# Attention values: the second half of the output copied by ScalarE and the sum moved to GpSimd

## The chip, the cores and the metric

The kernel runs on one NeuronCore of one Trainium2 chip. The metric is the device time of one execution in microseconds (us). Its engines are named as in the profile: PE (TensorE; PEld are its weight loads, which overlap the matmuls), DVE (VectorE), ACT (ScalarE), POOL (GpSimd) and SP (SyncE, which here issues DMAs).

## The reference

One layer of a backbone with two branches, on 1024 latent tokens (`x_sample`) and 128 context tokens (`x_prompt`), model width 1024. The change lies in the attention branch, of 8 heads. Each latent token reads 1152 keys (128 cached context keys and 1024 latent ones), and each context token reads the 128 keys of its own sequence:

```
s = einsum('bqhd,bkhd->bhqk', q_nope, k_nope) + einsum('bqhr,bkr->bhqk', q_rope, k_rope)
p = softmax(s.astype(float32) * scale, axis=-1).astype(v.dtype)
return einsum('bhqk,bkhd->bqhd', p, v)
...
y_a = (attn * silu(z_a)) @ w_a_out_l
merged = sigmoid(g_f) * y_f + sigmoid(g_a) * y_a
return x + gate * (merged @ w_out_l)
```

Around it stand the adaLN modulation, the input projection, a Fourier branch, the gated merge, the output projection and a final RMSNorm. All inputs and outputs are fp32.

## The kernel before

**Precision.** A matrix is split into a high and a low part in fp32r (`hi`/`lo`, `th`/`tl`, `kh`/`kl`). `mm3` (L122 to L127) makes a product of three matmuls: high by high (L123), high by low (L126), low by high (L127). The values' matrix V holds both of its parts side by side: `value_map` (L1044) writes the high part into columns 0 to 63 of a head's 128 and the low part into columns 64 to 127. A matmul with it as weights therefore gives 128 rows in PSUM, and rows 0 to 63 and 64 to 127 must be added to give the head's 64 output channels. The changed lines make this sum.

**Stages.** First come the modulation, the Fourier mixing and the input projection, then the Fourier output and the preparation of attention (L1059 to L1102). The attention stage is the loop of L1250 and runs from about 476 to 757 us in the profile. It is followed by the merge with the attention output map (`merge_part`, L1320) and the output projection with the final norm (L1360).

**Attention.** It takes 8 heads and 1152 query columns in 3 groups of 384 (`CH`). For each group and head:

- `q_chunk` (L1029): PE makes the queries, DVE multiplies them by the rotary table (`qf`, L1036), and POOL splits them in two instructions, `hi_pool` (L107) and `lo_pool` (L113), into the tile `q`.
- `Step.score` (L1123): PE makes 128 x 384 scores with `mm3`, DVE takes their minimum (L1131, L1136; scores are kept negated), and ACT makes the exponentials with their sums (`Step.exp`, L1142).
- `Group.trans` (L1155): PE transposes the exponentials (L1163), ACT copies the high part (`th`, L1164), and DVE takes the low part from PSUM (`tl`, L110).
- `Group.values` (L1176): PE accumulates nine key tiles, two matmuls each (L1183, L1184), in one PSUM bank `po`. After the ninth, ACT copies rows 64 to 127 to SBUF (`ob`, L1196) and DVE adds rows 0 to 63 from PSUM (L1197) into the tile `osb`, which two heads share.
- `finish` (L1204), after the odd head of a pair: DVE sums and inverts the softmax sums (L1210, L1212), POOL spreads the inverses over 64 columns in three instructions (L1217) which PE transposes (L1218), DVE multiplies the gate `za` by them (L1219) and by `osb` (L1220), and POOL splits `za` into `ath` (L107) and `atl` (L113). These are read by PE only in the merge.

`k_up` and `k_split` (L1003, L1017) make the next heads' keys in between: PE, two ACT copies (`kf`, L1013), and POOL's two instructions (`kh`, `kl`).

**Order.** The tokens in `HSEQ` (seven heads) and `LSEQ` (the last head) write down the order of scores, exponentials, transposes, values, queries and keys. The program is built with `schedule_with_timeline_sim=True` (L1537): when it is built, the order of the text is a priority, and each engine's list is laid down as a timing model plays the program. On the chip each engine then runs its list in order. So a later key split can stand ahead of an earlier `ath` in POOL's list.

**Buffers.** `ob`, `qf`, `kf` and the raw weights `hw` (L996, loaded by SP's queue) share four SBUF buffers of the pool `hpool` (L71, helper `H`, L90). PSUM has eight banks (`MM`, L102); scores, transposes, `po` and the keys all take theirs from these.

Of the kernel before, what the change touches and what calls it, by code (L numbers as in the profile page):

```python
# [13 lines left out]
ALU = mybir.AluOpType  # L14
# [7 lines left out]
CH = 384  # L22
# [42 lines left out]
def kernel(ctx: ExitStack, tc: tile.TileContext, a: dict):  # L65
    nc = tc.nc
    pe, act, dve, pool = nc.tensor, nc.scalar, nc.vector, nc.gpsimd
# [15 lines left out]
    def nm(s):  # L83
        cnt[0] += 1
        return f"{s}_{cnt[0]}"
# [4 lines left out]
    def H(shape, dt=F32, s="h"):  # L90
        return hpool.tile(shape, dt, tag="h", name=nm(s))
# [10 lines left out]
    def MM(tag="mm"):  # L102
        tag = tag if tag in banks else "mm"
        return psum.tile([P, 512], F32, tag=tag, bufs=banks[tag], name=nm(tag))
# [1040 lines left out]
    class Group:  # L1145
# [30 lines left out]
        def values(self, kt):  # L1176
            h, n = self.h, self.n
            if self.po is None:
                self.po = MM()
            po = self.po  # L1180
            th, tl = self.ts[kt // 3]
            i = kt % 3
            pe.matmul(po[:, 0:n], V[kt][:, h, :], th[:, i, 0:n], start=(self.nv == 0), stop=False)  # L1183
            pe.matmul(po[:, 0:n], V[kt][:, h, :], tl[:, i, 0:n], start=False, stop=(self.nv == 8))  # L1184
            self.nv += 1
            if i == 2:
                self.ts.pop(kt // 3)
            if self.nv == 9:
                if self.c == 2:
                    th, tl = self.ts.pop("c")  # L1190

                    tc.keep_in_program_order(pe.matmul(po[:, n:CH], V[9][:, h, :], th, start=True, stop=False))
                    pe.matmul(po[:, n:CH], V[9][:, h, :], tl, start=False, stop=True)
                e = h % 2
                ob = H([64, CH], s="ob")
                act.copy(ob, po[64:128, :CH])  # L1196
                dve.tensor_tensor(out=self.osb[64 * e : 64 * e + 64, self.c * CH : (self.c + 1) * CH],  # L1197
                                  in0=po[0:64, :CH], in1=ob, op=ALU.add)
                if e:
                    finish(h // 2, self.c, self.osb)  # L1200

# [2 lines left out]
    def finish(p, c, osb):  # L1204

        if c == 0:
            ath.append(U([P, NT], F32R, "ath"))
            atl.append(U([P, NT], F32R, "atl"))
        ssum = S([P, 2, 3], tag="ms", bufs=4)
        dve.tensor_reduce(out=ssum, in_=SSP[p % 2][:, :, 3 * c : 3 * c + 3, :], axis=AX.X, op=ALU.add)  # L1210
        rsm = S([P, 2, 3], tag="rsm", bufs=2)
        dve.reciprocal(rsm.rearrange("p a b -> p (a b)"), ssum.rearrange("p a b -> p (a b)"))  # L1212
        sl = slice(c * CH, (c + 1) * CH)
        ps = MM()
        for j in range(3):
            rb = S([P, 2, 64], tag="s512", bufs=4)
            hi_pool(rb, rsm[:, :, j : j + 1].to_broadcast([P, 2, 64]))  # L1217
            pe.transpose(ps[:, j * P : (j + 1) * P], rb.rearrange("p a b -> p (a b)"), ident)  # L1218
        dve.tensor_tensor(out=za[p][:, sl], in0=ps[:, :CH], in1=za[p][:, sl], op=ALU.mult)  # L1219
        dve.tensor_tensor(out=za[p][:, sl], in0=osb[:, sl], in1=za[p][:, sl], op=ALU.mult)  # L1220
        hi_pool(ath[p][:, sl], za[p][:, sl])
        lo_pool(atl[p][:, sl], za[p][:, sl], ath[p][:, sl])
# [318 lines left out]
```

## Time and profile before

| | |
|---|---|
| median of 3 runs | 914.64 us (914.39 to 915.91) |
| profiled execution | 914.43 us |
| its span, first to last instruction | 912.7 us |
| granted TensorE clock over the span | 0.998 of full speed |
| instructions | 15893 |

The span is 1.73 us shorter than the profiled execution's own time; that remainder lies before the first and after the last instruction. Durations of single instructions come from this one execution. In a row of the trace, "L1197 DVE TENSOR_TENSOR osb<-mm,ob" is the instruction of line 1197 on VectorE that writes `osb` and reads `mm` (a PSUM bank) and `ob`. A bracket such as "[0.80 <-DVE za L1220]" says that the engine stood idle for 0.80 us just before and that this instruction ended the wait. A line can be that of a helper (L107, L110, L113, L123 to L127), and then the tile's name tells which use it is.

### The profile page before, as it was taken

The page shows a single profiled execution, that of the slowest core. Times are in us where ns is not written, and L with a number is a line of the kernel's source. Part 1 is how long each engine was busy: PE and PEld are TensorE (multiplying, and loading weights), DVE is VectorE, ACT ScalarE, POOL GpSimd, SP SyncE. Part 2 cuts the span into 40 slices and gives each one's busy share as a digit, 9 for nine tenths or more (in the row PEclk, how much of TensorE's full clock was granted, in tenths as well). Part 3 has the DMA queues.
Part 4 walks back from the last instruction along what each step waited for, and adds up shares of the span by engine and source line. Part 5 has one row for each costly group of instructions (what it writes and reads, how often), then busy time and mean ns, then how long its engine had stood idle before and what let it go on. Part 6 is the DMA issues. An engine that isn't in the chain of part 4 may idle for free.

```text
span 912.7 us, 15893 instructions
## 1 busy us (share of the span) xinstructions
PE 887.8 (97%) x5886; PEld 843.6 (92%) x5886; DVE 603.8 (66%) x1305; ACT 471.0 (52%) x1269; POOL 270.7 (30%) x346
## 2 busy tenths in 40 slices
PE   4999999999999999999999999999999999999996
PEld 3889899999999999998899999999999989988885
DVE  2698963654444455467459889889889889965333
ACT  6784765533333334335138778778778781212111
POOL 0002203222222178520332362362353124212220
PEclk9999999999999999999999999999999999999999
DMA  9846563332222314579631000000000257342222
GB/s 365 340 158 215 187 232 125 117 114 111 100 108 109 127 58 155 200 227 366 230 140 52 7 8 1 10 6 1 10 7 1 64 213 270 101 163 90 97 103 78
DMA packets 35797, 115.59 MB, mean 127 GB/s; under 512 B 4484, under 2 KB 9348, under 8 KB 35720
## 3 DMA queue, kind: packets, MB, share of 16 engines
q1 hardware_dynamic: 31688, 105.94, 32.5%
q10 hardware_dynamic: 3168, 6.16, 1.8%
q0 software_dynamic: 864, 2.49, 0.9%
q8 instruction: 46, 0.75, 0.4%
q14 instruction: 31, 0.25, 0.1%
HBM read 81.74 MB, written 32.83 MB: 126 GB/s over the span
## 4 chain that ended last, share of the span: by engine, by line
PE 88%; DVE 4%; ACT 3%; DMA 2%; POOL 2%; issue 1%; SPq 0%; DVEq 0%; ACTq 0%; POOLq 0%
PE mm L123 24%; PE mm L126 23%; PE mm L127 23%; PE mm L1163 6%; PE mm L1184 3%; PE mm L1183 3%; PE mm L405 2%; PE mm L242 1%; PE mm L500 1%; DMA wr<-in_w_f_out 1%; PE mm L265 1%; DMA wut<-in_w_uT 1%; DVE tl L110 1%; DMA x<-in_x_sample 1%; DVE lo L110 0%
## 5 line engine op out<-in xcount | busy, mean ns | idle before, releaser
L1142 ACT ACTIVATE p<-mm,s 128x384 f32<-128x384 f32 x192 | 110.4, 590 | 11.9 <-DVE s L1136 11.6
L1131 DVE TENSOR_REDUCE s<-mm 128x1 f32<-128x384 f32 (+1 forms) x200 | 104.9, 541 | 12.4 <-PE mm L127 10.9
L110 DVE TENSOR_TENSOR tl<-mm,th 128x384 fp32r<-128x384 f32 (+1 forms) x216 | 102.0, 504 | 10.8 <-ACT th L1164 10.5
L127 PE MATMUL mm<-hTh,wp 128*128 128x288 f32 x352 | 103.9, 296 | 0.0
L123 PE MATMUL mm<-hTh,wp 128*128 128x288 f32 x352 | 103.8, 295 | 0.0
L126 PE MATMUL mm<-hTl,wp 128*128 128x288 f32 x352 | 103.8, 295 | 0.0
L1164 ACT CAST th<-mm 128x384 fp32r<-128x384 f32 (+1 forms) x216 | 89.1, 462 | 19.3 <-PE mm L1163 16.9
L1163 PE MATMUL mm<-c,p 128*128 128x128 f32 x576 | 93.9, 274 | 0.8 <-ACT s L1142 0.5
L127 PE MATMUL mm<-th,wp 128*128 128x288 f32 x264 | 77.9, 295 | 0.0
L126 PE MATMUL mm<-tl,wp 128*128 128x288 f32 x264 | 77.8, 295 | 0.0
L123 PE MATMUL mm<-th,wp 128*128 128x288 f32 x264 | 77.6, 295 | 0.0
L1163 PEld LDWEIGHTS mm<-c,p 128*128 128x128 f32 x576 | 71.0, 140 | 7.1 <-DVE tl L110 1.1
L1183 PE MATMUL mm<-th,v 128*128 128x384 f32 (+1 forms) x216 | 73.5, 344 | 0.0
L1184 PE MATMUL mm<-tl,v 128*128 128x384 f32 (+1 forms) x216 | 73.1, 342 | 0.2 <-DVE tl L110 0.2
L123 PE MATMUL mm<-kh,q 128*128 128x384 f32 x192 | 70.0, 365 | 1.2 <-POOL q L113 0.7
L123 PEld LDWEIGHTS mm<-hTh,wp 128*128 128x128 f32 x352 | 66.3, 188 | 0.0
L126 PEld LDWEIGHTS mm<-hTl,wp 128*128 128x128 f32 x352 | 66.3, 188 | 0.0
L127 PEld LDWEIGHTS mm<-hTh,wp 128*128 128x128 f32 x352 | 66.2, 188 | 0.0
L126 PE MATMUL mm<-kl,q 128*128 128x384 f32 x192 | 64.7, 337 | 0.0
L127 PE MATMUL mm<-kh,q 128*128 128x384 f32 x192 | 64.7, 337 | 0.0
L746 POOL TENSOR_TENSOR ws<-wr 128x512 f32<-128x512 f32 x11 | 14.4, 1306 | 153.5 <-DVE z L810 51.4
L810 DVE TENSOR_TENSOR z<-mm,u 128x288 f32<-128x288 f32 x66 | 29.8, 455 | 43.7 <-PE mm L127 43.5
(345 smaller groups left out, 2494.2 us busy)
## 6 DMA issues: line engine op xcount, KB each, us to landing
wr<-in_w_in SPq DMA_DIRECT2D x24, 512.0 KB, 4.2
x<-in_x_sample SPq DMA_DIRECT2D x16, 512.0 KB, 5.4
wada<-in_w_ada SPq DMA_DIRECT2D x16, 512.0 KB, 10.2
h_d<-hf SPq DMA_DIRECT2D x8, 576.0 KB, 2.9
gf_d<-z SPq DMA_DIRECT2D x8, 576.0 KB, 3.8
gfl<-gf_d SPq DMA_DIRECT2D x8, 576.0 KB, 5.0
mf_d<-mf SPq DMA_DIRECT2D x8, 576.0 KB, 3.8
gal<-ga_d SPq DMA_DIRECT2D x8, 576.0 KB, 3.7
```

What stands on the lines that cost most here:

```text
L110: dve.tensor_tensor(out=out, in0=x, in1=hi.bitcast(F32), op=ALU.subtract)
L123: i = pe.matmul(out, lh, rh, start=start, stop=False, skip_group_check=on)
L126: pe.matmul(out, lh, rl, start=False, stop=False, skip_group_check=on)
L127: pe.matmul(out, ll, rh, start=False, stop=stop, skip_group_check=on)
L405: pe.matmul(ps[:, j * P : (j + 1) * P], xt[4 * h + j][:, f * P : (f + 1) * P], diag[:, 4 * h + j, :], start=True, stop=True)
L810: dve.tensor_tensor(out=outs[i][:, sl], in0=ps, in1=t, op=ALU.add)
L1131: dve.tensor_reduce(out=self.nb if self.last else self.mx[:, kc : kc + 1], in_=ps[:, 0:n], axis=AX.X, op=ALU.min)
L1142: act.activation(self.p[:, kc * CH : kc * CH + n], self.ps[kc][:, 0:n], AF.Exp, scale=-1.0, bias=self.nb, accum_out=SSP[(self.h // 2) % 2] ...
L1163: pe.transpose(pt[:, j * P : (j + 1) * P], self.pr[j][:, kt * P : (kt + 1) * P], ident)
L1164: act.copy(th[:, i, 0:n], pt[:, 0:n])
L1183: pe.matmul(po[:, 0:n], V[kt][:, h, :], th[:, i, 0:n], start=(self.nv == 0), stop=False)
L1184: pe.matmul(po[:, 0:n], V[kt][:, h, :], tl[:, i, 0:n], start=False, stop=(self.nv == 8))
```

## The change

The two halves of `po` are both copied to SBUF by ACT, into `ob` and a new tile `oa` from the same four buffers, and the sum is a POOL instruction on two SBUF operands. Per group and head ACT runs one more instruction, DVE one fewer and POOL one more; there are 24 such groups. No DMA is added, removed or moved in the text.

```diff
@@ -1193,9 +1193,11 @@
                     pe.matmul(po[:, n:CH], V[9][:, h, :], tl, start=False, stop=True)
                 e = h % 2
                 ob = H([64, CH], s="ob")
+                oa = H([64, CH], s="oa")
                 act.copy(ob, po[64:128, :CH])
-                dve.tensor_tensor(out=self.osb[64 * e : 64 * e + 64, self.c * CH : (self.c + 1) * CH],
-                                  in0=po[0:64, :CH], in1=ob, op=ALU.add)
+                act.copy(oa, po[0:64, :CH])
+                pool.tensor_tensor(out=self.osb[64 * e : 64 * e + 64, self.c * CH : (self.c + 1) * CH],
+                                   in0=oa, in1=ob, op=ALU.add)
                 if e:
                     finish(h // 2, self.c, self.osb)
```

## Rows read from the trace of the kernel before

**Rows 1.** The page's first part: busy time of each engine over the span.

```profile
PE 887.8 (97%) x5886; PEld 843.6 (92%) x5886; DVE 603.8 (66%) x1305; ACT 471.0 (52%) x1269; POOL 270.7 (30%) x346
```

**Rows 2.** Busy time by stretch of attention: length, PE, PEld, DVE, ACT, POOL, clock, DMA.

```profile
476.00:546.00 70.00, 69.72 (x456) 67.51 (x455) 59.91 (x144) 55.88 (x169) 26.25 (x44) 1.00 0.10 38
...
686.00:757.00 71.00, 69.75 (x472) 66.38 (x472) 62.78 (x154) 54.34 (x166) 18.98 (x34) 1.00 0.31 109
sum 281.00, PE 278.88 PEld 269.16 DVE 242.97 ACT 221.51 POOL 104.42; mean PE 69.72 PEld 67.29 DVE 60.74 ACT 55.38 POOL 26.11
```

**Rows 3.** Waits of PEld, 476 to 757 us: total us, times, longest.

```profile
PEld mm L123 <- POOL q L113: 1.4, 3, 0.5
PEld mm L1163 <- DVE tl L110: 1.1, 4, 0.3
...
PEld mm L123 <- DVE osb L1197: 0.7, 1, 0.7
PEld mm L1184 <- DVE tl L110: 0.7, 2, 0.4
PEld mm L123 <- DVE tl L110: 0.5, 2, 0.3
```

**Rows 4.** Groups by line, 484 to 756 us: count, busy us, mean ns, idle before.

```profile
L113 POOL TENSOR_TENSOR kl<-kf,kh 64x384 fp32r<-64x384 f32 x18 | 18.1, 1005 | 0.8
...
L1197 DVE TENSOR_TENSOR osb<-mm,ob 64x384 f32<-64x384 f32 x24 | 13.1, 546 | 2.6 <-ACT ob L1196 2.2
...
L1196 ACT COPY ob<-mm 64x384 f32<-64x384 f32 x24 | 11.4, 477 | 20.9 <-PE mm L1184 18.8 <-PE mm L1193 1.8
```

**Rows 5.** The chain that ended last, 530 to 545 us: start, us, what.

```profile
533.26 0.55 DVE osb L1197
...
534.78 0.56 DVE za L1220
...
535.41 0.51 POOL ath L107
...
539.31 0.97 POOL q L113
...
540.40 0.41 PE mm L123
```

**Rows 6.** POOL in order of time: start, us, instruction, idle before it.

```profile
533.61 1.00 POOL L113 TENSOR_TENSOR kl<-kf,kh 64x384 fp32r<-64x384 f32 x1
535.41 0.51 POOL L107 TENSOR_SCALAR ath<-za 128x384 fp32r<-128x384 f32 x1 [0.80 <-DVE za L1220]
```

**Rows 7.** The chain that ended last, 737 to 757 us: start, us, what.

```profile
740.62 0.56 DVE osb L1197
741.20 1.80 ACT p L1142 x6
...
752.08 0.55 DVE osb L1197
752.66 0.44 DVE tl L110
753.14 0.39 PE mm L1184
```

**Rows 8.** A raw weight in time: its load on SP, its first use on POOL.

```profile
540.29 0.33 SPq L997 DMA_DIRECT2D hw<-in_w_uq  x1
...
546.58 0.40 POOL L107 TENSOR_SCALAR s<-hw 128x256 fp32r<-128x256 f32 x1
```

**Rows 9.** End of attention in time: POOL's last split, PE's first reader.

```profile
757.66 1.01 POOL L113 TENSOR_TENSOR atl<-za,ath 128x384 fp32r<-128x384 f32 x1
...
762.68 0.34 PE L123 MATMUL mm<-ath,whl 128*128 128x384 f32 x1
```

**Rows 10.** Two instructions that overlap in time, POOL's and DVE's.

```profile
755.09 1.01 POOL L113 TENSOR_TENSOR atl<-za,ath 128x384 fp32r<-128x384 f32 x1
...
755.52 0.98 DVE L1220 TENSOR_TENSOR za<-osb,za 128x384 f32<-128x384 f32 x1
```

## The prediction

> **What bounds the kernel now.** I read the page's busy times first: PE is busy 97% of the span and DVE 66% [rows 1]. These shares average over stages, so I cut out attention, where all changed instructions lie. There PE is busy 278.88 of 281.00 us and DVE 242.97, ACT 221.51 and POOL 104.42 [rows 2]. PE stands still for 2.1 us in the whole stage. DVE is the next fullest engine, but PE sets the time, and a change to the other three counts only where PE waits for them.
>
> These places are in the waits of PEld [rows 3]. Two kinds matter. Three times, once for each of the first three pairs of heads, PE waits about 0.47 us for POOL's split of the queries (1.4 us together). Eight times or so it waits for DVE: 1.1, 0.7 and 0.5 us for `tl`, and once 0.7 us for the `osb` sum that is to be moved.
>
> The chain that ended last shows what is late in each kind. Around 535 us it leaves PE and runs over DVE's `za` (L1219), the `osb` sum, `za` again (L1220), POOL's `ath`, the splits queued behind it, and POOL's split of q, which ends at 540.28 us and lets PE start at 540.40 [rows 5]. The changed sum lies on this chain, although nobody needs `ath` before the merge: it is POOL's queue that ties q to it. In the last head the chain runs on DVE and ACT, with two `osb` sums on it, at 740.62 and 752.08 us [rows 7].
>
> **The change, part by part.** There are 24 sums. DVE loses 24 x 0.546 = 13.1 us. ACT gains 24 copies of the same shape as `ob`, 24 x 0.477 = 11.4 us. POOL gains 24 sums of two SBUF operands; the nearest row, a 64x384 instruction with two SBUF operands, takes 1.005 us, so 24.1 us [rows 4]. The stage's totals become DVE 229.9, ACT 232.9 and POOL 128.5 us, all far under PE's 278.88 [rows 2]. The totals therefore cost nothing; PE is the cover. What counts is order in the queues.
>
> *The three q splits.* POOL now stands idle 0.80 us ahead of `ath` [rows 6], and from there to the end of q it is nearly full, so the new 1.005 us can use 0.80 us of idle time and pushes the rest by 0.20 us. In detail: `ob` and `oa` should be in SBUF at about 533.3 us; the sum comes before `finish` and the later key splits in the text, so I put it at 533.6, where `kl` stands now, ending at 534.6; `kl` then ends at 535.6 instead of 534.6. DVE's `za` (L1220), 534.78 now, finds its `osb` at 534.6 and is not late; `ath` comes at 535.6 instead of 535.41. PE already waits at this place, so all of it counts: 3 x 0.20 = +0.6 us. The ends are -1.4 us (the waits for q vanish, since the sum's 0.55 us leaves DVE's chain) and 3 x 1.005 = +3.0 us (the idle time does not help). I take +0.6 because it is worked out from the idle row nearest to the place.
>
> *The last head.* The sum at 752.08 us stands directly ahead of the `tl` for which PE waits at 753.14 [rows 7]. Without it `tl` starts up to 0.55 us earlier, and of PEld's wait there, 0.4 us [rows 3], I take all: -0.4 us. The ends are -0.55 us and +0.5 us (ACT's new copy of 0.477 us delays a `th` as much). The other sum, at 740.62, releases the bank for which PE waits 0.7 us, but ACT's exponentials follow it on the chain at 741.20 and end 1.80 us later, so PE would come earlier only to wait there: 0, with -0.7 us as the other end. The remaining waits for `tl`, 1.1 + 0.7 + 0.5 - 0.4 = 1.9 us [rows 3], are spread over `tl` instructions that have no sum ahead of them: 0, with -1.9 us as the end.
>
> *Waits added.* POOL's sum waits for ACT; behind it in POOL's queue wait key splits, q splits and the spread inverses, which PE transposes. DVE's `za` (L1220) now waits for POOL; behind it wait `qf`, `tl` and minima. Both are priced at the q splits above, the one place where POOL is full; at the other groups POOL, busy 128.5 of 281 us, leaves room. The bank `po` is freed by a second copy of 0.477 us on ACT instead of a 0.546 us sum on DVE [rows 4], so not later: 0.
>
> *Four shared buffers.* A second tile per group, held until POOL's sum ends, can make the next `kf`, `qf` or `hw` wait for a buffer. The load of `hw` is issued on SP's queue at 540.29 us and first read at 546.58 [rows 8], a margin of several sums, and SP's queue has nothing else urgent in these heads. I take 0; without that margin, one sum's length at each of the three places, which is the upper end above again.
>
> *The end of the stage.* The last group's path grows by 0.477 and by 1.005 - 0.546, about 0.9 us. Its `atl` ends at 758.67 and PE comes to the part that reads it at 762.68 [rows 9]; 4.0 us cover it: 0.
>
> **The sum.** +0.6 - 0.4 = +0.2 us on the profiled execution's 914.43 us: **914.6 us**. That execution lies 0.21 us under the median of the runs shown, 914.64, so the forecast is no change. All lower ends together give 914.43 - 1.4 - 0.55 - 0.7 - 1.9 = 909.9, all upper ends 914.43 + 3.0 + 0.5 = 917.9 us. A measurement of this kernel can tell about 0.2%, 1.8 us, from no change.
>
> **The rivals.** *Faster: DVE was the real brake.* All waits of PEld that name DVE, 1.1 + 0.7 + 0.7 + 0.5 = 3.0 us [rows 3], vanish and q is not later: 911.4 us. For it speaks that DVE is the fullest engine after PE and loses 5% of its work. Against it, in the last head ACT holds the chain as long as DVE does [rows 7], and ACT gets fuller. On what is to be gained at most, the page "Perfetto Trace Analysis" of the Trainium skill, section Identifying the Most-Contended Engine, says that matmul busy time misjudges how near TensorE is to its limit and that the busy share of weight loads should be taken. By that rule the slack would be 281.00 - 269.16 = 11.8 us instead of 2.1 [rows 2] and the bound about 902.6 us; the waits in the trace do not bear that out, since those that name DVE come to 3.0 us.
>
> *Slower: POOL's queue.* The sum is put behind `kl` at 533.61 to 534.61 [rows 6] and ends at 535.6; `za`, `ath` and q follow a whole sum later. PE is late there already, so it decides from the first tenth. With three full sums and no gain in the last head: 914.43 + 3.0 = 917.4 us. For it: q is split right behind `ath` and `atl` [rows 5]. Against it: the order of the text puts the sum ahead.
>
> *Slower or no change: a collision.* Where the sum goes first, `kl` runs beside `za` (L1220). The one such overlap in the trace took 0.98 us instead of 0.56 and ended 0.40 us after POOL's instruction did [rows 5, 10]. At 535.6 + 0.40 = 536.0, `ath` is about 0.7 us later than now: 914.43 + 3 x 0.7 - 0.4 = 916.1 us. The page "SBUF — State Buffer" of the Trainium skill, section Who interferes with whom, gives the same rule: a VectorE instruction with two SBUF inputs and a GpSimd one that reads SBUF exclude each other; the overlap shown agrees.
>
> *Slower: another order.* The lists are laid down anew when the program is built, and every engine's order after the first sum may differ. In the last head's stretch, which has another written order, PE idles 71.00 - 69.75 = 1.25 us, in the first 70.00 - 69.72 = 0.28 [rows 2]. If the first three stretches fell to that: 914.43 + 3 x 0.97 = 917.3 us.
>
> **How the numbers follow.** Chances: forecast 0.47, faster by DVE 0.20, POOL's queue 0.17, collision 0.08, another order 0.08. The collision at 916.1 lies near the 0.2% bound, and I give half of it to each side: faster 0.20, same 0.51, slower 0.29. The range reaches from 912.3, two thirds of the way to the DVE rival, to 917.6, which takes in the POOL queue and the new order; some 0.2 is left outside, about half on each side.
>
> **What would show it.** Right: in attention DVE near 230, ACT near 233, POOL near 128 us and PE's busy time unchanged at 278.9; `osb` on POOL at about 1.0 us; the three waits for q near 0.7 us each; the wait for `tl` near 753 us gone. Wrong: waits for q above 1 us each or for `za` on DVE (slower), PE's waits for DVE gone without new ones (faster), or PE's idle time spread over new places, which would mean that the order of the lists and not a price decides.

## The result and the profile after

The changed kernel takes **922.30 us** (median of 4 runs, 921.28 to 923.03), the kernel before 914.51 us (4 runs, 913.45 to 915.91): a ratio of **1.0085** with a 95% interval of 1.0073 to 1.0097, so 7.8 us slower. The forecast was 914.6 us, no change, with a range from 912.3 to 917.6 us. The measured time lies 4.7 us above that range, and above the price of every rival.

First the page's busy times after the change, which answer to [rows 1]:

```profile
PE 892.5 (97%) x5886; PEld 844.7 (92%) x5886; DVE 593.5 (64%) x1281; ACT 478.8 (52%) x1293; POOL 297.9 (32%) x370
```

The groups by line (count, busy us, mean ns, idle time before) answer to [rows 4]:

```profile
L1199 POOL TENSOR_TENSOR osb<-oa,ob 64x384 f32<-64x384 f32 x24 | 24.1, 1005 | 41.4 <-ACT oa L1198 40.8
L1198 ACT COPY oa<-mm 64x384 f32<-64x384 f32 x24 | 11.3, 473 | 0.6
L1222 DVE TENSOR_TENSOR za<-osb,za 128x384 f32<-128x384 f32 x12 | 7.0, 582 | 3.5 <-POOL osb L1199 3.2
```

The change does what it says, at the durations forecast: the sum takes 1005 ns on POOL (forecast 1.005 us), the copy 473 ns (0.477). Neither totals nor durations explain the loss. The attention stage by stretches answers to [rows 2] (columns as there):

```profile
476.00:546.00 70.00, 69.00 (x444) 65.68 (x443) 57.01 (x135) 56.43 (x169) 29.72 (x46) 1.00 0.11 39
...
686.00:757.00 71.00, 68.92 (x457) 65.77 (x458) 60.15 (x145) 56.34 (x174) 26.01 (x40) 1.00 0.22 74
sum 281.00, PE 275.88 PEld 263.17 DVE 230.52 ACT 226.21 POOL 124.97; mean PE 68.97 PEld 65.79 DVE 57.63 ACT 56.55 POOL 31.24
```

The clock is the same, and PE is busy 3.0 us less in the same stretch, its weight loads 6.0 us less. To see how long attention itself takes, one needs two marks that mean the same in every kernel. I take the first start of the reduction L1136 and the first start of PE's matmul on `ath` (L123). The view of one line and of one tile, of the kernel before:

```profile
L1136 DVE TENSOR_REDUCE s<-s x64: 144/148/157, 480.0 to 742.7; 128x1 f32<-128x3 f32 x64
L123 PE MATMUL mm<-ath,whl x96: 333/336/387, 754.2 to 807.6; 128*128 128x384 f32 x96
```

And of the kernel after:

```profile
L1136 DVE TENSOR_REDUCE s<-s x64: 143/148/158, 480.6 to 749.9; 128x1 f32<-128x3 f32 x64
L123 PE MATMUL mm<-ath,whl x96: 331/338/426, 761.4 to 814.1; 128*128 128x384 f32 x96
```

Attention takes 754.2 - 480.0 = 274.2 us before and 761.4 - 480.6 = 280.8 us after: +6.6 us. This length stands in the table of the experiments below as "attention".

What PE waits for now, in the waits of PEld from 476 to 757 us, which answer to [rows 3]:

```profile
PEld mm L1163 <- ACT s L1013: 2.0, 3, 0.9
PEld mm L123 <- POOL q L107: 1.9, 3, 0.7
PEld mm L1163 <- DVE tl L110: 1.2, 3, 0.4
PEld mm L123 <- ACT p L1142: 0.8, 3, 0.3
```

The first is new: three times, once in each of the first three pairs of heads, a transpose waits for ScalarE's copy of the context keys. That instruction was not changed. ScalarE in order of time shows why it is late, first before:

```profile
535.18 0.98 ACT L1013 COPY kf<-mm 64x384 f32<-64x384 f32 x2 [1.49 <-PE mm L127]
536.18 0.86 ACT L1164 CAST th<-mm 128x384 fp32r<-128x384 f32 x2
...
538.05 0.26 ACT L1013 COPY kf<-mm 64x128 f32<-64x128 f32 x1
```

and after:

```profile
536.61 0.97 ACT L1013 COPY kf<-mm 64x384 f32<-64x384 f32 x2 [0.74 <-PE mm L127]
538.54 0.26 ACT L1013 COPY kf<-mm 64x128 f32<-64x128 f32 x1 [0.96 <-PE mm L1163]
538.83 0.26 ACT L1013 COPY s<-mm 64x128 f32<-64x128 f32 x1
539.11 1.24 ACT L1164 CAST th<-mm 128x384 fp32r<-128x384 f32 x3
```

**The list is another one.** Before, two copies `th` (and two exponentials) stood between the large and the small key copies; now the small ones come first, ScalarE stands idle 0.96 us, and the `th` wait behind them, although by the trace the transposes that two of them copy had ended at 536.83 us. (The Trainium skill, "PSUM — Partial Sum Buffer", section Engine vs sequencer instructions, says that the queues of ScalarE, VectorE and GpSimd are strictly first in, first out; the 0.96 us agrees.) The row puts the idle time down to a transpose (L1163); in e3 and e10 below the same wait is put down to the last matmul of the context keys (L127), which here ends 0.36 us before the copy starts, so part of the 0.96 us stays unexplained. POOL's list moved too. Its chain after, from the view of the chain that ended last, answers to [rows 5]:

```profile
536.14 1.00 POOL osb L1199
...
538.54 0.98 POOL kl L113
539.53 0.48 POOL ath L107
540.01 0.98 POOL kl L113
540.99 0.53 POOL kch L107 x2
541.51 0.98 POOL atl L113
542.50 0.49 POOL q L107
542.99 0.04 issue
543.03 0.45 PE mm L123
```

Before, `atl` and the high part of q stood ahead of five key splits that they now stand behind. In the lists of the built programs, 403 of PE's 5694 places, 143 of VectorE's 1281, 58 of ScalarE's 1038 and 50 of POOL's 346 hold another instruction than before (copies and sum of the change left out), all of them in attention or at its very end.

### The profile page after: what moved, and what is told of

It reads as the page before. It is cut to its first block, busy times and chain, and to the rows that moved or that the text cites. A ratio compares the mean times of both kernels' runs of the same rounds, so it can differ in the third digit from the quotient of the medians.

```text
span 920.4 us, 15929 instructions
## 1 busy us (share of the span) xinstructions
PE 892.5 (97%) x5886; PEld 844.7 (92%) x5886; DVE 593.5 (64%) x1281; ACT 478.8 (52%) x1293; POOL 297.9 (32%) x370
## 4 chain that ended last, share of the span: by engine, by line
PE 86%; POOL 3%; ACT 3%; DVE 3%; DMA 2%; issue 1%; SPq 0%; DVEq 0%; POOLq 0%; ACTq 0%
PE mm L123 23%; PE mm L126 22%; PE mm L127 22%; PE mm L1163 5%; PE mm L1184 3%; PE mm L1183 3%; PE mm L405 2%; PE mm L242 1%; POOL kl L113 1%; PE mm L500 1%; PE mm L265 1%; DMA wr<-in_w_f_out 1%; DMA wut<-in_w_uT 1%; ACT p L1142 1%; POOL kh L107 1%
## 5 line engine op out<-in xcount | busy, mean ns | idle before, releaser
L127 PE MATMUL mm<-hTh,wp 128*128 128x288 f32 x352 | 103.9, 296 | 0.0
L123 PE MATMUL mm<-hTh,wp 128*128 128x288 f32 x352 | 103.8, 295 | 0.0
L1163 PE MATMUL mm<-c,p 128*128 128x128 f32 x576 | 95.1, 273 | 2.7 <-ACT s L1013 1.3
L1163 PEld LDWEIGHTS mm<-c,p 128*128 128x128 f32 x576 | 71.6, 140 | 9.2 <-ACT s L1013 2.0
L127 PE MATMUL mm<-th,wp 128*128 128x288 f32 x264 | 77.9, 295 | 0.0
L123 PE MATMUL mm<-th,wp 128*128 128x288 f32 x264 | 77.6, 295 | 0.0
L1184 PE MATMUL mm<-tl,v 128*128 128x384 f32 (+1 forms) x216 | 74.0, 347 | 0.0
L123 PE MATMUL mm<-kh,q 128*128 128x384 f32 x192 | 70.1, 365 | 2.3 <-POOL q L107 1.1
L123 PEld LDWEIGHTS mm<-hTh,wp 128*128 128x128 f32 x352 | 66.3, 188 | 0.0
L127 PEld LDWEIGHTS mm<-hTh,wp 128*128 128x128 f32 x352 | 66.2, 188 | 0.0
L127 PE MATMUL mm<-kh,q 128*128 128x384 f32 x192 | 64.0, 338 | 0.0
L127 PE MATMUL mm<-hi,ml 128*128 128x512 f32 (+1 forms) x152 | 58.0, 384 | 0.0
```

The lines of the kernel that those rows point to most:

```text
L123: i = pe.matmul(out, lh, rh, start=start, stop=False, skip_group_check=on)
L127: pe.matmul(out, ll, rh, start=False, stop=stop, skip_group_check=on)
L1163: pe.transpose(pt[:, j * P : (j + 1) * P], self.pr[j][:, kt * P : (kt + 1) * P], ident)
```

## The experiments

Three theories. **O**: the order laid anew when the program is built costs it. **P**: GpSimd's sum and its queue cost it in any order. **R**: `oa` holds one of the four shared buffers until the sum ends, and later copies wait.

To part instructions and order, a kernel can fix each engine's list. Runs e1 to e3 and all from e5 on do it so, with the list of every engine stored in `ORDER`; it adds dependencies that give an order and no semaphore:

```diff
+    for x, y in zip(own, own[1:]):
+        tc.add_manual_dep(ins[y], ins[x].name, info, reason="order")
```

These kernels have 57 or 58 more lines ahead of the changed code, so L1163 is L1220 or L1221 there, L123 is L180 or L181. No run fixes the old order unchanged. The nearest to it show no price of the fixing: e3 (the changed kernel's order fixed, 1.0072 against 1.0085 with overlapping intervals) and e17 (the old order fixed but for three places, 0.9996).

| run | instructions | order | median us | ratio [95%] | attention us |
|---|---|---|---|---|---|
| before | old | old | 914.51 | | 274.2 |
| after | changed | new | 922.30 | 1.0085 [1.0073, 1.0097] | 280.8 |
| e1 | changed | old | 918.89 | 1.0042 [1.0027, 1.0057] | 277.7 |
| e2 | old | new | 922.46 | 1.0083 [1.0068, 1.0098] | 281.6 |
| e3 | changed, `oa` apart | new | 921.68 | 1.0072 [1.0057, 1.0087] | 280.8 |
| e4 | two copies, DVE sum | a third one | 934.00 | 1.0211 [1.0194, 1.0228] | 293.5 |
| e5 | old | old, PE new | 923.31 | 1.0088 [1.0073, 1.0103] | 281.7 |
| e6 | old | old, ACT new | 922.88 | 1.0090 [1.0075, 1.0105] | 283.0 |
| e7 | old | old, ACT and POOL new | 926.20 | 1.0130 [1.0114, 1.0146] | 286.1 |
| e8 | two copies, DVE sum | old | 917.28 | 1.0029 [1.0019, 1.0039] | 277.3 |
| e9 | changed | new, key copies back | 920.60 | 1.0068 [1.0055, 1.0082] | 280.9 |
| e10 | old | old, key copies early | 916.73 | 1.0028 [1.0017, 1.0038] | 276.9 |
| e11 | changed | old, `oa` later | 917.16 | 1.0031 [1.0020, 1.0043] | 277.6 |
| e12 | DVE copy, POOL sum | old | 916.17 | 1.0022 [1.0013, 1.0031] | 276.2 |
| e13 | changed | new, ACT and POOL pieces back | 917.47 | 1.0031 [1.0020, 1.0042] | 276.5 |
| e14 | old | new in the middles only | 918.16 | 1.0039 [1.0025, 1.0053] | 277.7 |
| e15 | old | new elsewhere only | 919.25 | 1.0051 [1.0036, 1.0066] | 279.1 |
| e16 | changed | new, middles old | 919.14 | 1.0051 [1.0036, 1.0066] | 278.9 |
| e17 | old | old, best middle | 914.35 | 0.9996 [0.9987, 1.0005] | 273.6 |
| e18 | changed | old, best middle | 918.23 | 1.0039 [1.0026, 1.0053] | 278.0 |

Each ratio is to the runs of the kernel before that belong to it, whose medians were 914.27 to 915.15 us; differences in the text are to these.

### Order or instructions: e1, e2, e3, e4

e1 is the changed kernel with `ORDER` taken from the kernel before, `oa` directly behind `ob`. e2 is the kernel before with the changed kernel's `ORDER`.

> The changed kernel's instructions in the order of the lists of the kernel before: every engine's list is fixed; oa stands directly behind ob in ScalarE's list, and the sum in GpSimd's list at the place where the trace of before has reached 0.5 us after ob's end. The kernel before takes 914.5 us, the changed one 922.3. Theory O (the order laid anew when the program is built costs the 7.8 us, the new instructions nothing): 914 to 915.5 us. Theory P (GpSimd's sum of 1.0 us and what queues behind it cost it, in any order): 920 to 923 us. Theory R (oa shares four buffers with ob, qf, kf and hw and is held until GpSimd's sum ends, so that later kf copies wait and with them the PSUM banks that PE needs): 920 to 923 us, with weight loads of PE at L1163 waiting for ScalarE's copy L1013.

> The instructions of the kernel before (one copy ob, VectorE's sum) in the order of the lists of the changed kernel; VectorE's sum is placed at the first place after ob's end by the changed kernel's trace. Theory O (the order costs it): 920 to 923 us. Theories P and R (GpSimd's sum, or the shared buffers, cost it): 913.5 to 916 us. With the run of the changed instructions in the old order this makes a table of two orders by two sets of instructions.

e2 decides on the whole: the old instructions in the new order take 922.46 us, as slow as the changed kernel. But the equal totals have unequal parts. VectorE at the 52nd of the 64 reductions L1136, in the seventh head, in the changed kernel:

```profile
699.93 0.16 DVE L1136 TENSOR_REDUCE s<-s 128x1 f32<-128x3 f32 x1
```

and in e2:

```profile
696.65 0.16 DVE L1194 TENSOR_REDUCE s<-s 128x1 f32<-128x3 f32 x1
```

The kernel before reaches it at 693.45 us. From the first reduction to this one the changed kernel loses 5.9 us against before and e2 3.9; from there to the first matmul on `ath` they lose 0.7 and 3.5. So up to the seventh head the order alone makes 3.9 of the 5.9 us and the new instructions 2.0 more; behind it the order costs the old instructions 3.5 us and the changed ones hardly anything. That the totals agree is in part chance, and why the last part differs is open. These are single executions, though e3 and e9 repeat the changed kernel's two parts (6.0 and 0.6 to 0.7 us).

e1 is no clean success for O: in the old order the new instructions cost 3.7 us, which O said they would not; 918.89 us lies in no theory's range. The wait that was new after the change is in e2 as well, without any POOL sum. Idle times of PEld in e2, in order of time:

```profile
536.93 0.31 PEld L1221 LDWEIGHTS mm<-c,p 128*128 128x128 f32 x3 [0.60 <-ACT s L1071]
```

(L1071 there is L1013.) e3 takes R alone, with a buffer of its own for `oa`; the room comes from a tile of an earlier stage:

```diff
-                t1 = S([P, 2, 2, 8], tag="s128", bufs=4)
+                t1 = S([P, 2, 2, 8], tag="s128", bufs=3)
...
-                oa = H([64, CH], s="oa")
+                oa = S([64, CH], tag="oa", bufs=1, s="oa")
```

> The changed kernel in its own order, with one difference: oa has a buffer of its own (one, of spool) instead of a place among the four that ob, qf, kf and hw share. Theory R (kf, qf, ob or hw wait for a buffer until GpSimd's sum ends): 914.5 to 917 us, and the wait of PE's weight loads at L1163 for ScalarE's L1013, 2.0 us in the changed kernel, is gone. Theories O and P: 921 to 923.5 us, and that wait stays.

Attention is 280.8 us as before the edit, and the wait stays (PEld's waits in e3):

```profile
PEld mm L1221 <- ACT s L1071: 1.8, 3, 0.6
```

R falls. (`ob`, which POOL's sum now also holds longer, still shares the four buffers in e3; e2 covers that, since it has no such sum and shows the same wait.) e4 leaves the sum on VectorE and lets the lists be laid anew:

```diff
-                pool.tensor_tensor(out=self.osb[...
+                dve.tensor_tensor(out=self.osb[...
```

> Both halves are copied by ScalarE as in the changed kernel, but the sum of oa and ob stays on VectorE (two SBUF operands); lists laid anew. GpSimd is as before. Theory P (GpSimd's sum): 913.5 to 916 us. Theory R in the form that any second tile of the shared four costs it: 918 to 923 us; in the form that only its release by GpSimd's late sum does: 914 to 916 us. Theory O: anything from 913 to 923 us, for another order again.

934.00 us, without any sum on POOL: P cannot explain that. It is outside what R said, and outside what I had allowed O.

### Which engine's list: e5, e6, e7, e8

In e5 to e7 the kernel before takes single lists from the new order. e8 is e4 with every list in the old order.

> The kernel before in its own order, but TensorE's list alone in the changed kernel's order. The whole new order costs 7.3 us (the run of the old instructions in it took 922.5 us). Theory O-PE (what costs is TensorE's order: the transposes of a group stand one place earlier against the values' matmuls, and the scores' third matmuls are put off to behind the values): 920 to 923 us. Theory O-lists (it is the order of the copies and splits on ScalarE and GpSimd, and TensorE's list only answers it): 914 to 917 us.

> The kernel before in its own order, but ScalarE's list alone in the changed kernel's order: in each odd head the two copies of the context keys (L1013, k_up of the fourth part) stand ahead of three of the copies of transposes they stood behind. Theory O-ACT (the copies that free PSUM banks for the next transposes come late): 918 to 923 us, with weight loads at L1163 waiting for L1013 by 1.5 us or more. Otherwise: 914 to 916 us.

> The kernel before in its own order, but the lists of ScalarE and GpSimd together in the changed kernel's order (GpSimd splits the low part of the next head's queries behind all six key splits instead of in the middle of them). Theory O-lists (these two lists cost it): 920 to 923 us, GpSimd's share being the difference to the run with ScalarE's list alone. Theory O-PE (TensorE's list costs it): 914 to 917 us.

> Both halves copied by ScalarE, the sum of oa and ob on VectorE at the old sum's place in its list, every list in the order of the kernel before. With the lists laid anew this took 934.0 us, and the changed kernel in the old order took 918.9. Theory O: the 19 us are the order's, so 915 to 919 us here. If ScalarE's 24 copies of 0.47 us, which hold the bank longer and stand ahead of copies of transposes, are what the changed instructions cost in the old order, 918 to 919; if it is GpSimd's sum, 914.5 to 916. If the instructions themselves cost the 19 us: above 930.

PE's list alone costs 8.3 us, ScalarE's alone 7.9, ScalarE's and POOL's together 11.2, all of them 7.3 (e2). e5 ends 0.3 us above the range that blames PE's list, e6 inside the one that blames ScalarE's, and e7 above both of its ranges; the sign that e6 was to show, waits at L1163 for L1013, is missing: PE waits for `th` instead (3.6 us). So the question was badly put: one foreign list among old ones costs as much as a full new set, and the sums of such runs mean nothing. That the lists are laid to fit one another would explain it, but is argued only.

e8 is the strongest witness for O: the same instructions as e4, 917.28 instead of 934.00 us; against their own runs of the kernel before, 2.3 instead of 18.9 us, so 16.6 us are order alone. It also prices ScalarE's second copy with what hangs on it (VectorE's sum must wait for `oa` and reads two SBUF tiles): 2.3 us, between the two answers that its forecast gave for the copy and for GpSimd's sum. Where it goes is seen in ScalarE's list of e8, in order of time:

```profile
592.16 0.47 ACT L1255 COPY oa<-mm 64x384 f32<-64x384 f32 x1
592.53 0.47 ACT L1221 CAST th<-mm 128x384 fp32r<-128x384 f32 x1
```

with PEld behind it:

```profile
593.06 0.19 PEld L1240 LDWEIGHTS mm<-th,v 128*128 128x128 f32 x1 [0.31 <-ACT th L1221]
```

Before, `th` started right behind `ob`, and PE did not wait here:

```profile
591.62 0.47 ACT L1196 COPY ob<-mm 64x384 f32<-64x384 f32 x1
592.12 0.48 ACT L1164 CAST th<-mm 128x384 fp32r<-128x384 f32 x1
```

Now `oa` is between, and PE waits 0.31 us.

### The knot in the odd heads: e9 to e12

```diff
 ScalarE, odd head, groups of the second 384 columns (e9, from the new order)
-kf(keys 3)  s(keys 3)  th(3)  th(4)  th(5)
+th(3)  th(4)  kf(keys 3)  s(keys 3)  th(5)
 GpSimd
-kch  kch  atl  q_hi
+atl  q_hi  kch  kch
```

e10 makes ScalarE's move the other way in the kernel before, and nothing else. e11 puts `oa` of e1 behind the next `th`, in 17 of 24 groups. e12 is e1 with `dve.tensor_copy(oa, po[0:64, :CH])` in place of `act.copy`.

> The changed kernel in its own order but for one place in each of the first three pairs of heads: ScalarE's two copies of the context keys (L1013, fourth part of k_up), which stand ahead of the copies th of key tiles 3 and 4, go back behind them, and in GpSimd's list atl and the high part of q go ahead of the two context key splits that these copies feed. In the changed kernel's trace ScalarE stands idle 0.96 us at the first of these copies (538.54 us) with the two th behind it. Theory O-ACT (this idle time is what the new order costs): about 3 x 0.9 = 2.7 us or more is given back, 917.5 to 919.7 us, and the waits of PE's weight loads at L1163 for L1013 are gone. Rival (the new order costs it in many places, this one being covered elsewhere): 921 to 923 us.

> The kernel before in its own order, but the same two copies of the context keys put ahead of the copies th of key tiles 3 and 4 on ScalarE, in the first three pairs of heads: six instructions moved, nothing else. ScalarE's whole list in the new order took 922.9 us. Theory O-ACT: 919 to 923 us, with an idle time of ScalarE ahead of L1013 in each pair. Rival: 914.5 to 916.5 us.

> The changed kernel in the old order (918.9 us), but oa stands one place later on ScalarE, behind the next copy th, in the 17 of 24 groups where th is what follows. In the run in the old order PE's weight loads waited for th 1.4 us in attention against 0.5 before, and once in each odd head 0.31 us for the th directly behind oa. Theory (the rest of 3.7 us is ScalarE's second copy standing ahead of th): 916.5 to 917.5 us. Rival (it is GpSimd's sum, which then comes later still): 918.5 to 920 us.

> VectorE copies the second half into oa at the old sum's place in its list, ScalarE has its one copy as before, GpSimd makes the sum; every list in the order of the kernel before. Theory (ScalarE's second copy is the rest of 3.7 us; the sum on GpSimd costs nothing): 914.5 to 916 us. Rival (GpSimd's sum, through VectorE's za and the shared buffers, is the rest): 917 to 919 us.

**e9 missed.** The waits for L1013 are gone, but attention is 280.9 us, as long as before the move. The profiled execution is 1.6 us shorter, and 1.3 us of that lie ahead of attention (L1136 starts at 479.3 instead of 480.6 us). PE waits for the splits of q in their place:

```profile
PEld mm L181 <- POOL q L165: 2.5, 3, 0.9
PEld mm L185 <- POOL q L171: 1.9, 3, 0.6
```

So my theory that ScalarE's list alone was the brake fell: behind it stood POOL's, equally late. **e10** came out between its two answers, 0.2 us above the rival's range: 2.5 us for six moved instructions, with PE waiting 1.1 us for `th` in each pair. **e11** has the median that was expected, but it lies 2.9 us above its own runs of the kernel before and e1 3.7 above its own, the two intervals overlap, and attention is no shorter (277.6, 277.7): inconclusive. **e12** prices POOL's sum without ScalarE's copy: 1.9 us. That is between its two ranges, and the theory that the sum costs nothing fails. PE in order of time there shows what I had misread before the change:

```profile
540.35 0.42 PE L180 MATMUL mm<-kh,q 128*128 128x384 f32 x1 [0.24 <-DVE tl L167]
...
541.41 0.45 PE L184 MATMUL mm<-kh,q 128*128 128x384 f32 x1
```

and the weight load of the second of them:

```profile
541.41 0.19 PEld L184 LDWEIGHTS mm<-kh,q 128*128 128x128 f32 x1 [0.43 <-POOL q L170]
```

L180 is L123, the product that reads only the high part of q; L184 is L127, which reads the low part.

### The two lists together, and where the rest lies: e13 to e16

e13 is e9 with POOL's whole piece back:

```diff
 GpSimd, odd head (e13, from the new order)
-sum kh kh kl ath kl kch kch atl q_hi kcl kcl q_lo
+sum kh ath atl q_hi kh kl q_lo kch kch kl kcl kcl
```

For e14 to e16 the "middle" of an odd head (from its last scores to the second scores of the next head) takes all engines' lists from one order and the rest from the other.

> The changed kernel in its own order, with ScalarE's two copies of the context keys back behind the th of key tiles 3 and 4 as in the run before, and GpSimd's piece between the sum and the next q back in the old order as well, so that both splits of q stand ahead of the context key splits; three places each. In the run with the copies alone moved back, PE's weight loads waited 2.5 us at L123 and 1.9 us at L127 for the splits of q, in the three pairs. Theory (one knot on ScalarE and GpSimd: q and th held up by the context keys): these waits fall to under 1.5 us together, 916.5 to 919 us. Rival (TensorE's own order there costs by itself): 919.5 to 921 us.

> The kernel before in its own order, but in the middle of each odd head of the first three pairs (from its last scores to the second scores of the next head) all engines' lists are in the changed kernel's order. From the starts of the same reductions in the traces of before and of the old instructions in the new order, this stretch loses 1.5, 0.7 and 0.75 us in the three pairs. Theory (the loss sits in this middle): 917 to 918.5 us. Rival (it sits elsewhere and the middle only shows it): 914 to 915.5 us.

> The kernel before in the changed kernel's order everywhere in attention except in those three middles, where the old order stands. Theory (the middle holds 3 of the 7.3 us, the passage from an even to an odd head about 0.3 us each and the last head some 1.5 to 3): 916.5 to 919.5 us. Rival (all of it elsewhere): 921 to 923 us.

> The changed kernel in its own order, but in those three middles all engines' lists are in the old order. By the starts of the same reductions in its trace and in that of before, the middles hold 2.0, 1.2 and 1.2 us of the changed kernel's loss in attention. Theory (middle): 917 to 919 us. Rival: 921 to 923 us.

**e13** met its forecast: 917.47 us, attention 276.5. Against the changed kernel's 280.8, two pieces of list at three places give back 4.3 us. No wait for q is left at that place; what remains of PEld's idle time from 533 to 545 us is one row:

```profile
537.33 0.31 PEld L1221 LDWEIGHTS mm<-c,p 128*128 128x128 f32 x3 [0.45 <-DVE tl L168]
```

e14 and e15 put the old instructions' loss at 3.8 us in the middles and 4.9 elsewhere (together 8.6 against 7.3 at once), e16 gives back 3.0 of 7.8 us. e13 to e15 lie within their forecasts, e16 just above. PEld's waits elsewhere are many and small and are not broken down here.

### A better middle: e17, e18

In that place PE waits 0.45 us in e13 and 0.30 + 0.17 + 0.47 = 0.94 us before the change. e17 gives the kernel before e13's middle, e18 gives it to e1.

> The kernel before in its own order, except that in the three middles TensorE and VectorE have the changed kernel's order and ScalarE has it with the context key copies behind the th of key tiles 3 and 4; GpSimd's list is the old one. Theory (this middle is better than the old one by 0.94 - 0.45 = 0.49 us a pair): 912.5 to 913.8 us, faster than the kernel before. Rival (the wait comes back behind it): 914 to 916 us.

> The changed kernel's instructions in the old order (918.9 us) with that same middle; GpSimd's list is that of the run in the old order, oa stands directly behind ob. Theory: 1.5 us better than that run, 916.5 to 917.7 us, since ScalarE's second copies and GpSimd's sums cost what they cost there. Rival (the two savings do not add, or the sum is late for the next reader): 918 to 920 us.

The rivals hold: e17 is 0.9996 of the kernel before, no difference that can be told. The waits of L123 at the splits of q are gone from its PEld, but those for `tl` at L1184 are 1.6 us against 0.7, and attention is 273.6 us against 274.2. e18 keeps a loss of 3.6 us. No version beat the kernel before.

## Why the prediction was wrong, point by point

**The step that failed: the lists were taken as fixed.** The sum of the parts put the new instruction "at 533.6, where `kl` stands now" and let the rest move along behind it. In truth the lists of PE, DVE, ACT and POOL were all laid anew. The rival "another order" named this, with a chance of 0.08 and a price of 2.9 us taken from the last head; e2 shows 7.3 us, and e4 against e8 shows that 16.6 is possible. Why this order came out can only be argued: in the text the tiles of `th` for key tiles 3 to 5 are drawn from the same pool behind `ath`, `atl` and q, so a sum that delays those on POOL in the timing model may also delay `th` there, and the key copies pass it. No run shows that.

**A copy costed at nothing.** ScalarE's second copy was costed at 0 because `po` comes free no later; that it delays a `th` was named only as the upper end in the last head. The trace of before has a `th` directly behind `ob` at 592.12 us, so the copy stands ahead of it: e8 measures 2.3 us for it and what hangs on it. This wrong term is smaller than the first, but with it the forecast "no change" would fail in the old order as well (e1: 3.7 us).

**The three q splits: right size, wrong reading.** I priced POOL's sum at 0.20 us a pair. In e12, where every list is the old one, it is close to that. VectorE around the 52nd reduction L1136 before:

```profile
693.45 0.16 DVE L1136 TENSOR_REDUCE s<-s 128x1 f32<-128x3 f32 x1
```

and in e12:

```profile
694.09 0.16 DVE L1193 TENSOR_REDUCE s<-s 128x1 f32<-128x3 f32 x1
```

The fourth reduction starts at 485.02 and 485.00 us; 0.66 us are lost over three pairs, 0.22 each. But the wait of 0.47 us [rows 3, 5], which I took for POOL's low part of q, was not that: L123 does not read the low part, and in PE's built list a wait for `tl` of key tile 5 stands directly ahead of it. Both ended at about 540.3 us, and the profile named the other. In e1 the low part of q is written from 542.58 us on:

```profile
542.58 0.99 POOL L170 TENSOR_TENSOR q<-qf,q 128x384 fp32r<-128x384 f32 x1
```

That ends 0.7 us after PE has gone on, and the wait is 0.47 us as ever, now put down to `kl`:

```profile
542.91 0.19 PEld L180 LDWEIGHTS mm<-kh,q 128*128 128x128 f32 x1 [0.47 <-POOL kl L170]
```

In e12 the low part does hold PE, at L127, by 0.43 us. The size agreed by luck.

**The last head and the end of the stage.** Forecast -0.4 and 0. To see it, VectorE must have lost the sum in the old order, as in e1 (in e12 a copy of the same length stands in its place). There the wait of 0.41 us for the last `tl` is gone as forecast, and the 0.67 us for the `osb` sum become 0.45 us for `oa`. But other waits come in, at another `tl` and at the merge's first matmul on `ath`:

```profile
746.87 0.31 PEld L1220 LDWEIGHTS mm<-c,p 128*128 128x128 f32 x3 [0.43 <-DVE tl L167]
...
759.36 0.19 PEld L180 LDWEIGHTS mm<-ath,whl 128*128 128x128 f32 x1 [0.50 <-DVE za L1278]
```

(L1278 is L1219.) From the 52nd reduction (697.82 us) to that matmul e1 takes 61.6 us against 60.8 before: +0.8 instead of -0.4, so the mechanism was there, but other waits took more than its gain. In e12, 0.66 of the 2.0 us that attention grew lie in the first three pairs, so 1.3 lie behind them. Its PEld waits name one 0.9 us wait of the transposes of the spread inverses (L1218) for POOL, a queue that I had called free there.

**The slack.** I set aside the rule of the Trainium skill ("Perfetto Trace Analysis", section Identifying the Most-Contended Engine) that matmul busy time misjudges how near TensorE is to its limit and weight loads should be taken. The stretches 476 to 757 us of e1, where attention is 3.5 us longer:

```profile
sum 281.00, PE 278.77 PEld 266.14 DVE 232.05 ACT 229.13 POOL 126.94; mean PE 69.69 PEld 66.53 DVE 58.01 ACT 57.28 POOL 31.74
```

PE is as busy as in [rows 2] (278.88), PEld 3.0 us less. The loss shows in PEld alone; on that the rule agrees with the trace.

**What held:** the four shared buffers cost nothing (e3: attention unchanged), totals and durations came as forecast, and POOL's queue did turn out slow, but by its order and not by a full queue. (A slip without effect: two thirds of the way from 914.6 to 911.4 us is 912.5, not 912.3.)

**The account.** Of the 6.6 us that attention grew, 4.3 come back when pieces of ScalarE's and POOL's lists are put back at three places (e13); the old instructions in the new order lose 3.9 us up to the seventh head (e2). What the 2.3 us left in e13 are is open. In the old order the instructions cost as much: 1.9 us by median for the sum (e12), 2.3 for the copy (e8), 3.7 for both (e1). But the new order outside the middles costs the old instructions 4.9 us (e15), and no run parts the two.

## What to carry to other kernels

Where lists are laid by a model when the program is built, an edit's price has two parts, and the second can be the larger: compare the lists of before and after first, and run the old instructions in the new order before blaming an instruction, comparing stretch by stretch and not the totals alone. Before believing a named wait, ask whether the waiting instruction reads that tile at all. An added copy on an engine with much idle time still delays whatever stands behind it in the queue: look at the next instruction, not at the total.

## What the runs showed that was not expected

The stages ahead of attention, with the same instructions in the same lists, end at different times: L1136 starts at 478.7 us in e11 and at 481.7 in e1. Part of the difference between two medians can lie there, as with e9 and e11; its cause is open. And a POOL instruction that starts just behind a VectorE one on two SBUF operands takes longer: the instruction that spreads the inverses takes 0.29 us alone and 0.66 us beside `za` (L1220) in e12, where `za` had started 0.05 us earlier and kept its 0.56 us. In the changed kernel two splits `kh`, the first of them 0.05 us behind `za` (537.17 us), take 1.35 us together, where one takes 0.51 before. The forecast had this collision the other way round, with `za` as the one that is held up; in its row [rows 10] POOL's instruction had started first.
